# First RMS norm of a two-layer trunk: squares on VectorE, row scaling on ScalarE, and the high part of h written directly

## The chip, the cores and the metric

The kernel runs on one core of a Trainium2 chip. The metric is device time in microseconds (us) of one execution, median over runs. A core has a matrix engine (TensorE, in the profile PE, with its weight loads as PEld), VectorE (DVE), ScalarE (ACT), GpSimd (POOL), and a queue engine (SyncE, SP) that issues the loads here. Each engine works through its own list of instructions strictly in order; between engines they wait on semaphores. PSUM banks hold what TensorE writes; everything else is in SBUF.

## The reference

The model is one gated-MLP layer followed by one latent-attention layer, over 256 tokens of width 2048. The change touches the norm ahead of each sub-layer:

```python
def rms_norm(x, g):
    xf = x.astype(jnp.float32)
    y = xf * lax.rsqrt(jnp.mean(xf * xf, axis=-1, keepdims=True) + EPS)
    return (y * g.astype(jnp.float32)).astype(x.dtype)

def ada_mod(c, w, b):
    return (jax.nn.silu(c) @ w + b)[:, None, :]
...
    shift, scale, gate = jnp.split(ada_mod(c, ada_w[i], ada_b[i]), 3, axis=-1)
    h = rms_norm(x, norm_g[i]) * (1.0 + scale) + shift
    if i < N_A_LAYERS:
        out = gmlp_mixer(h, a_w_in[i], a_ln_g[i], a_ln_b[i], a_w_s[i], a_b_s[i], a_w_out[i])
...
    x = x + gate * out
```

`gmlp_mixer` begins with `h @ w_in`, a 2048 by 12288 product. The keys and values and the second layer take `h` in the same form.

## The kernel before

**Products.** Every matrix product is made in three passes of a reduced float format (fp32r): an operand is split into a high part `hi` and a rest `lo`, and hi by hi, lo by hi and hi by lo are summed. A weight piece of 1 MB (`raw`, two blocks of 128 rows by 1024 columns) is loaded by SP, cast to `hi` on ScalarE (L164) and subtracted to `lo` on VectorE (L166). It feeds 24 matmuls of 512 columns (L328): two row blocks, two token tiles, two halves of the columns, three passes.

**The left operand h.** `Norm.h` takes one block of 128 features of the transposed, normalised x (`xT`, in the second layer `zT`), applies the adaLN scale and shift as per-partition columns (L289, into a scratch tile `h` of which there are two), casts it to the high part (L290; the tile is called hh in the first layer, gh in the second, shi for the keys and values) and lets VectorE write the low part (L291; hl, gl, slo). It runs 52 times: 16 blocks in the first norm, 20 in the second (the first four blocks in two halves of 128 tokens), 16 for the keys and values.

**adaLN columns.** `Ada.step` loads 1 MB of transposed adaLN weights (`araw`) and VectorE multiplies it with silu(c), held as `s_b` on all partitions, and sums along the row (L191, one custom instruction and a short one that reads the accumulator). One step gives one column of 128 values. `modulate(k)` runs a shift step and a scale step and then `Norm.h` for block k, so a block of h costs 2 MB of loads. For the scale VectorE adds one and multiplies by the norm's weight (L195). The first steps, for blocks 0 and 1, are called sh0, sc0, sh1, sc1 below, and those for block 2 sh2 and sc2.

**The first norm.** `Norm.rows` handles one token tile of 128 rows after the other. ScalarE squares four quarters of a row with running sums (L145), VectorE adds the four sums (L158) and scales and shifts the mean (L139), GpSimd raises it to the power -0.5 (L140, tile `rs`), VectorE multiplies the four quarters with it (L262), and TensorE transposes each quarter (`flip`, L251) into a bank `px` from which ScalarE copies it to `xT` (L253). Two banks serve this. The two token tiles are called `x_83` and `x_85` in the lists below.

**Buffers and order.** Loads of `raw` and `araw` share four buffers of 1 MB: SP issues a load when VectorE has finished with the tile that was in its buffer. SP's order is that of the source; on the other engines a planner in the compiler sets the order of the instructions by costs of its own, so an edit in one place can move instructions elsewhere. The startup works in stages of 1, 1, 2, 2, 2 weight pieces per block of columns and calls `modulate` for the next stage between them.

**The second norm** (`norm1`) works otherwise: the transposes come first, and the row scales are applied to `zT` by VectorE from a transposed copy (`finish`, a PE transpose of `rs` at L275, and `scale`, L284; `zrb` is its copy in SBUF at L279). `early1` does blocks 0 to 3 for each token tile, `late1` the rest.

## Time and profile before

| what | value |
|---|---|
| median of 3 runs | 1158.75 us (1155.67 to 1169.34) |
| the profiled execution | 1158.37 us, of which the span from first to last instruction is 1156.6 us |
| granted TensorE clock, mean | 0.988 |
| TensorE busy | 1120.1 us (97% of the span) |
| VectorE busy | 958.4 us (83%) |
| ScalarE busy | 623.3 us (54%) |
| GpSimd busy | 53.9 us (5%) |
| DMA engines, share of the span on the loads' queue | 80% |

A row of a timeline gives the start in us, the time taken in us (from the start of the first to the end of the last where several are merged), the engine, the line, the operation, the tile written and the tiles read, their shapes and the count; in brackets stands how long the engine had been idle and what it waited for. A row of the windows gives the busy time of each engine in that stretch, then the granted TensorE clock, the busy share of the DMA engines, and GB/s.

### The profile page before, as it was taken

How to read it: one execution, taken by the hardware profiler on the slowest of the kernel's cores; microseconds unless marked ns; L12 is line 12 of the kernel's file. 1: busy time of each engine (PE TensorE's matmuls, PEld its weight loads, DVE VectorE, ACT ScalarE, POOL GpSimd, SP SyncE). 2: the span in 40 equal slices, each digit the busy share in tenths (PEclk: the TensorE clock that was granted, in tenths of full speed). 3: DMA queues.
4: the chain of work that ended last, by engine and by line, in shares of the span. 5: the costliest groups of instructions: out<-in, count | busy, mean ns of one | idle time of the engine just before them, and what ended most of it. 6: DMA issues, size and time to landing. Idle time of an engine off the chain costs nothing.

```text
span 1156.6 us, 14438 instructions
## 1 busy us (share of the span) xinstructions
PE 1120.1 (97%) x5148; PEld 919.3 (79%) x5148; DVE 958.4 (83%) x1389; ACT 623.3 (54%) x1150; POOL 53.9 (5%) x70
## 2 busy tenths in 40 slices
PE   7998999999999999999999989989999999999997
PEld 4777788888788888878888878868888788887886
DVE  6799999978998987897898888879876657687896
ACT  6744344456754434444445454457647688784332
POOL 0000000001210000000000000000000132120000
PEclk8999999999999999999999999989999999999999
DMA  9999888988898898989989989968986555245784
GB/s 354 350 344 344 309 316 329 339 295 299 301 350 338 320 345 317 357 308 348 361 306 339 335 293 339 326 246 328 359 297 196 200 155 165 84 163 199 259 301 188
DMA packets 80298, 338.30 MB, mean 292 GB/s; under 512 B 5729, under 2 KB 10209, under 8 KB 63457
## 3 DMA queue, kind: packets, MB, share of 16 engines
q1 hardware_dynamic: 79074, 335.29, 80.0%
q10 hardware_dynamic: 1152, 2.10, 0.6%
q8 instruction: 40, 0.66, 0.2%
q14 instruction: 32, 0.26, 0.1%
HBM read 335.26 MB, written 2.10 MB: 292 GB/s over the span
## 4 chain that ended last, share of the span: by engine, by line
PE 71%; DMA 10%; DVE 10%; issue 4%; ACT 4%; POOL 0%; SPq 0%; DVEq 0%; ACTq 0%; POOLq 0%
PE pm L328 58%; DMA araw<-in_ada_wT 4%; DVE lo L166 4%; PE pk L328 4%; PE pq L328 3%; DMA araw<-in_kv_ada_wT 3%; DVE araw L191 2%; ACT hi L164 1%; PE pS L845 1%; DMA raw<-in_a_w_in 1%; PE pS L844 1%; PE pmix L556 1%; ACT sq L145 1%; DMA lnb<-in_a_ln_b 1%; DVE v L467 1%
## 5 line engine op out<-in xcount | busy, mean ns | idle before, releaser
L164 ACT CAST hi<-raw 128x1024 fp32r<-128x1024 f32 (+2 forms) x376 | 382.2, 1029 | 403.2 <-PE pm L328 278.9
L166 DVE TENSOR_TENSOR lo<-raw,hi 128x1024 fp32r<-128x1024 f32 (+2 forms) x376 | 443.8, 1195 | 78.8 <-ACT hi L164 77.7
L191 DVE CUSTOM_DVE_ANT_0 araw<-araw,s_b,vec 128x2048 f32<-128x2048 f32 (+1 forms) x128 | 274.7, 2148 | 54.1 <-DMA araw<-in_ada_wT 33.6
L328 PE MATMUL pm<-lo,hh 128*128 128x512 f32 x768 | 251.9, 395 | 6.7 <-DVE lo L166 6.5
L328 PE MATMUL pm<-hi,hh 128*128 128x512 f32 x768 | 243.5, 394 | 6.6 <-ACT hh L290 3.5
L328 PE MATMUL pm<-hi,hl 128*128 128x512 f32 x768 | 247.9, 392 | 0.0
L328 PEld LDWEIGHTS pm<-lo,hh 128*128 128x128 f32 x768 | 143.8, 189 | 40.3 <-DVE lo L166 11.4
L328 PEld LDWEIGHTS pm<-hi,hh 128*128 128x128 f32 x768 | 145.0, 189 | 38.6 <-DVE v L467 4.1
L328 PEld LDWEIGHTS pm<-hi,hl 128*128 128x128 f32 x768 | 144.9, 189 | 30.8 <-DVE hl L291 0.3
L328 PE MATMUL pm<-lo,shi 128*128 128x512 f32 (+1 forms) x320 | 94.2, 371 | 2.3 <-DVE lo L166 2.3
L328 PE MATMUL pm<-hi,shi 128*128 128x512 f32 (+1 forms) x320 | 94.3, 374 | 0.9 <-ACT shi L164 0.9
L328 PE MATMUL pm<-hi,slo 128*128 128x512 f32 (+1 forms) x320 | 94.2, 372 | 0.0
L328 PEld LDWEIGHTS pm<-lo,shi 128*128 128x128 f32 x320 | 58.4, 188 | 12.6 <-DVE lo L166 2.7
L328 PEld LDWEIGHTS pm<-hi,shi 128*128 128x128 f32 x320 | 58.0, 188 | 11.0 <-ACT shi L164 1.3
L328 PEld LDWEIGHTS pm<-hi,slo 128*128 128x128 f32 x320 | 58.0, 188 | 10.0
L328 PE MATMUL pm<-hi,gh 128*128 128x512 f32 x160 | 52.9, 402 | 1.2 <-ACT kn L732 1.2
L328 PE MATMUL pm<-hi,gl 128*128 128x512 f32 x160 | 54.0, 400 | 0.0
L328 PE MATMUL pm<-lo,gh 128*128 128x512 f32 x160 | 53.5, 401 | 0.0
L328 PE MATMUL pk<-hi,latkv 128*128 128x512 f32 x128 | 43.9, 411 | 0.0
L328 PE MATMUL pm<-lo,ybh 128*128 128x512 f32 x128 | 43.2, 395 | 0.0
L328 PE MATMUL pm<-hi,ybl 128*128 128x512 f32 x128 | 43.0, 395 | 0.0
L328 PE MATMUL pm<-hi,ybh 128*128 128x512 f32 x128 | 42.9, 402 | 0.0
(178 smaller groups left out, 1240.4 us busy)
## 6 DMA issues: line engine op xcount, KB each, us to landing
araw<-in_ada_wT SPq DMA_DIRECT2D x96, 1024.0 KB, 6.5
raw<-in_a_w_in SPq DMA_DIRECT2D x96, 1024.0 KB, 6.6
raw<-in_a_w_out SPq DMA_DIRECT2D x32, 1024.0 KB, 7.2
araw<-in_kv_ada_wT SPq DMA_DIRECT2D x32, 1024.0 KB, 6.9
raw<-in_b_w_in SPq DMA_DIRECT2D x16, 1024.0 KB, 6.2
raw<-in_b_w_out SPq DMA_DIRECT2D x16, 1024.0 KB, 5.4
raw<-in_kv_w_ukv SPq DMA_DIRECT2D x8, 1024.0 KB, 5.6
raw<-in_b_w_uq SPq DMA_DIRECT2D x8, 768.0 KB, 4.9
```

The costliest lines, as they stand in the source:

```text
L145: nc.scalar.activation(j, src, AF.Square, scale=scale, accum_out=dst)
L164: nc.scalar.copy(hi, src)
L166: nc.vector.tensor_tensor(out=lo, in0=src, in1=hi.bitcast(F32), op=ALU.subtract)
L191: nc.vector.tensor_tensor_reduce(out=t[:, c], in0=t[:, c], in1=s_b[:, c], scale=1.0, scalar=acc, op0=ALU.mult, op1=ALU.add, accum_out=dst)
L328: nc.tensor.matmul(ps[i][:, :widths[i]], lhsT=lt, rhs=rhs[:, offs[i]:offs[i] + widths[i]], start=(first and c == 0 and which == 0 and rhs ...
L467: nc.vector.tensor_tensor(out=p, in0=ps, in1=p, op=ALU.add)
L556: nc.tensor.matmul(pmix[:, j * 256:(j + 1) * 256], lhsT=wsh["T"][:, g, :], rhs=piece(vt[i], t, n)[:, j * 256:(j + 1) * 256], start=True, s ...
L844: nc.tensor.matmul(pS[:, c0:c1], lhsT=qT[:, j, t * P:(t + 1) * P], rhs=kT[:, j, 0:nk], start=True, stop=False)
L845: nc.tensor.matmul(pS[:, c0:c1], lhsT=qrT[pb:pb + DR, t * P:(t + 1) * P], rhs=krT[pb:pb + DR, 0:nk], start=False, stop=True)
```

## The change

In `Norm.rows` both token tiles are now handled together. The squares of a whole row of 2048 are formed and summed by one VectorE instruction per tile, of the same kind as the adaLN step: it reads the row tile twice, as both inputs, and writes the products to a tile `sq` that nobody reads. The sum of four partial sums goes away. The rows are scaled on ScalarE, with the GpSimd result as a per-partition scale, quarter by quarter and both tiles in turn, and each quarter is transposed as before.

In `Norm.h` the high part is written first and straight from `xT` or `zT` with scale and shift; `h` itself is written by a second instruction of the same form, where a cast stood before. The low part is `h` minus the high part as before. This holds for all 52 uses.

```diff
-        def rows(self, t):
-
+        def rows(self):
+
+            r = []
+            for t in range(NT):
+                nc.vector.tensor_tensor_reduce(out=slot("sq"), in0=self.xt[t], in1=self.xt[t], scale=1.0, scalar=0.0, op0=ALU.mult, op1=ALU.add, accum_out=self.st[t][:, 0:1])
+                r.append(rstd_sum(self.st[t], 1, D))
             for q in range(4):
-                self.sums(t, q)
-            r = rstd_sum(self.st[t], 4, D)
-            for q in range(4):
-                x = self.xt[t][:, q * 512:(q + 1) * 512]
-                nc.vector.tensor_scalar_mul(x, x, r)
-                self.flip(t, q)
+                for t in range(NT):
+                    x = self.xt[t][:, q * 512:(q + 1) * 512]
+                    nc.scalar.activation(x, x, AF.Identity, scale=r[t])
+                    self.flip(t, q)
...
         def h(self, n, k, hi, lo, t0=0, t1=S):
             src = self.ts[k // 8][:, (k % 8) * S + t0:(k % 8) * S + t1]
+            scale, bias = ada["sc" + n].col[:, k:k + 1], ada["sh" + n].col[:, k:k + 1]
+            nc.scalar.activation(hi, src, AF.Identity, scale=scale, bias=bias)
             h = scratch([P, S], "h", "h")[:, :t1 - t0]
-            nc.scalar.activation(h, src, AF.Identity, scale=ada["sc" + n].col[:, k:k + 1], bias=ada["sh" + n].col[:, k:k + 1])
-            nc.scalar.copy(hi, h)
+            nc.scalar.activation(h, src, AF.Identity, scale=scale, bias=bias)
             return nc.vector.tensor_tensor(out=lo, in0=h, in1=hi.bitcast(F32), op=ALU.subtract)
...
-    for t in range(NT):
-        norm0.rows(t)
+    norm0.rows()
```

In the lists that follow, the lines of the changed kernel are two or three higher from L264 on (the scaling of the rows is L264 there, the squares L259, the high part L291, h L293, the low part L294). ISA is the custom VectorE instruction and the read of its accumulator.

**VectorE at the start, before:**

```order
L158 TENSOR_REDUCE ss_131<-st_121 128x1
L139 TENSOR_SCALAR rs_133<-ss_131 128x1
L262 TENSOR_SCALAR x_83<-x_83,rs_134 128x512 x4
L158 TENSOR_REDUCE ss_173<-st_122 128x1
L139 TENSOR_SCALAR rs_175<-ss_173 128x1
L191 ISA araw,col_sh_111<-araw,s_b,vec 128x2048
L191 ISA col_sh_111 128x1
L262 TENSOR_SCALAR x_85<-x_85,rs_176 128x512 x4
L191 ISA araw,col_sc_112<-araw,s_b,vec 128x2048
L191 ISA col_sc_112 128x1
L195 SCALAR_TENSOR_TENSOR col_sc_112<-col_sc_112,vec 128x1
L166 TENSOR_TENSOR lo<-raw,hi 128x1024 x2
```

And in the changed kernel, up to the first low part of h:

```order
L259 ISA sq,st_121<-x_83 128x2048
L259 ISA st_121 128x1
L139 TENSOR_SCALAR rs_125<-st_121 128x1
L259 ISA sq,st_122<-x_85 128x2048
L259 ISA st_122 128x1
L139 TENSOR_SCALAR rs_131<-st_122 128x1
L191 ISA araw,col_sh_111<-araw,s_b,vec 128x2048
L191 ISA col_sh_111 128x1
L191 ISA araw,col_sc_112<-araw,s_b,vec 128x2048
L191 ISA col_sc_112 128x1
L195 SCALAR_TENSOR_TENSOR col_sc_112<-col_sc_112,vec 128x1
L294 TENSOR_TENSOR hl_193<-h,hh_191 128x256
```

The second square stands directly behind the small operation (L139) whose result GpSimd waits for. The list goes on before, from the two low parts of the first weight piece, as

```order
L166 TENSOR_TENSOR lo<-raw,hi 128x1024 x2
L191 ISA araw,col_sh_111<-araw,s_b,vec 128x2048
L191 ISA col_sh_111 128x1
L291 TENSOR_TENSOR hl_209<-h,hh_207 128x256
L191 ISA araw,col_sc_112<-araw,s_b,vec 128x2048
```

and changed as

```order
L166 TENSOR_TENSOR lo<-raw,hi 128x1024
L191 ISA araw,col_sh_111<-araw,s_b,vec 128x2048
L191 ISA col_sh_111 128x1
L166 TENSOR_TENSOR lo<-raw,hi 128x1024
L191 ISA araw,col_sc_112<-araw,s_b,vec 128x2048
```

so the adaLN step sh1 has moved between the two low parts of the first weight piece, and the low part of h ahead of both.

**ScalarE at the start, before:**

```order
L128 ACTIVATE s_b<-pc 128x512
L145 ACTIVATE sq,st_121<-x_83 128x512 x4
L128 ACTIVATE s_b<-pc 128x512 x2
L145 ACTIVATE sq,st_122<-x_85 128x512 x4
L128 ACTIVATE s_b<-pc 128x512
L253 COPY xT_119<-px 128x4x128 x2
L253 COPY xT_120<-px 128x4x128 x2
L253 COPY xT_119<-px 128x4x128 x2
L253 COPY xT_120<-px 128x4x128 x2
L164 CAST hi<-raw 128x1024 x2
L289 ACTIVATE h<-xT_119,col_sh_111,col_sc_112 128x256
L290 CAST hh_207<-h 128x256
```

and changed:

```order
L128 ACTIVATE s_b<-pc 128x512 x3
L264 ACTIVATE x_83<-x_83,rs_126 128x512 x4
L128 ACTIVATE s_b<-pc 128x512
L253 COPY xT_119<-px 128x4x128
L264 ACTIVATE x_85<-x_85,rs_132 128x512 x4
L253 COPY xT_119<-px 128x4x128 x3
L253 COPY xT_120<-px 128x4x128
L291 ACTIVATE hh_191<-xT_119,col_sh_111,col_sc_112 128x256
L293 ACTIVATE h<-xT_119,col_sh_111,col_sc_112 128x256
L164 CAST hi<-raw 128x1024 x2
L253 COPY xT_120<-px 128x4x128 x3
```

The last quarter of `s_b`, which the first adaLN step needs whole, now stands behind the four scalings of the first tile; the first block of h stands ahead of the first weight cast and of three transposed quarters.

**ScalarE at the second norm, before,** from the first copy of the row scales on:

```order
L279 COPY zrb<-px 128x128
L289 ACTIVATE h<-zT_232,col_sh_114,col_sc_115 128x128 x2
L253 COPY zT_233<-px 128x4x128
L290 CAST gh_5866<-h 128x128 x2
L279 COPY zrb<-px 128x128
L289 ACTIVATE h<-zT_232,col_sh_114,col_sc_115 128x128 x2
L290 CAST gh_5866<-h 128x128 x2
L289 ACTIVATE h<-zT_232,col_sh_114,col_sc_115 128x128 x2
L290 CAST gh_5866<-h 128x128 x2
L289 ACTIVATE h<-zT_232,col_sh_114,col_sc_115 128x128 x2
L290 CAST gh_5866<-h 128x128 x2
```

and changed:

```order
L281 COPY zrb<-px 128x128
L291 ACTIVATE gh_5850<-zT_216,col_sh_114,col_sc_115 128x128
L293 ACTIVATE h<-zT_216,col_sh_114,col_sc_115 128x128
L291 ACTIVATE gh_5850<-zT_216,col_sh_114,col_sc_115 128x128
L293 ACTIVATE h<-zT_216,col_sh_114,col_sc_115 128x128
L291 ACTIVATE gh_5850<-zT_216,col_sh_114,col_sc_115 128x128 x2
L253 COPY zT_217<-px 128x4x128
L293 ACTIVATE h<-zT_216,col_sh_114,col_sc_115 128x128 x2
L281 COPY zrb<-px 128x128
L291 ACTIVATE gh_5850<-zT_216,col_sh_114,col_sc_115 128x128 x4
L291 ACTIVATE shi<-zT_216,col_shk,col_sck 128x256 x2
L293 ACTIVATE h<-zT_216,col_sh_114,col_sc_115 128x128 x4
```

High parts no longer need one of the two `h` tiles, so they run ahead; the four `h` of the second token tile now stand behind six high parts, two of which (shi) are for the keys and values. SP's order is the same in both kernels.

## The prediction

> **What bounds the kernel now.** I read the windows by stage first, then the chain of waits, then the timelines of VectorE, ScalarE and GpSimd over the first 36 us.

> ```profile
> 0.00:43.00 43.00, 34.15 (x113) 22.81 (x114) 28.64 (x40) 28.59 (x54) 2.48 (x11) 0.92 0.94 363
> 43.00:75.00 32.00, 32.00 (x143) 26.50 (x142) 27.46 (x30) 20.23 (x31) 0.00 (x0) 1.00 0.95 346
> 75.00:124.00 49.00, 42.86 (x174) 33.09 (x172) 47.65 (x58) 18.28 (x23) 0.00 (x0) 0.97 0.89 326
> 124.00:400.00 276.00, 274.45 (x1214) 226.22 (x1215) 246.78 (x281) 147.07 (x205) 15.00 (x19) 1.00 0.89 322
> ...
> 5.99 2.51 ACT sq L145 x8
> 124.08 135.99 PE pm L328 x598
> ```

> The columns after the length are PE, PEld, VectorE, ScalarE and GpSimd, then clock, DMA share and GB/s. From 43 to 75 us TensorE is never idle; from 75 to 124 VectorE is (47.65 of 49 us busy) what it waits for; from 124 on the chain is matmuls. So the end moves with TensorE's stream: whatever the first 40 us gain or lose is passed on, unless VectorE's slack (28.64 of 43 us busy) takes it up. The first 18 us of the chain are what the change rewrites; the first squares on ScalarE (5.99) head it.

> **The first norm.** These rows carry the start:

> ```profile
> 1.61 0.42 SPq L114 DMA_DIRECT2D x<-in_x  x1
> x<-in_x SPq DMA_DIRECT2D x1, 1024.0 KB, 6.9
> 8.45 1.05 ACT L128 ACTIVATE s_b<-pc 128x512 f32<-128x512 f32 x2
> 8.77 0.15 DVE L139 TENSOR_SCALAR rs<-ss 128x1 f32<-128x1 f32 x1
> 9.01 0.56 POOL L140 TENSOR_TENSOR rs<-rs,nhalf 128x1 f32<-128x1 f32 x1 [7.17 <-DVE rs L139]
> 9.60 1.67 DVE L262 TENSOR_SCALAR x<-x,rs 128x512 f32<-128x512 f32 x4 [0.68 <-POOL rs L140]
> 11.86 0.58 ACT L128 ACTIVATE s_b<-pc 128x512 f32<-128x512 f32 x1
> 12.47 2.35 DVE L191 CUSTOM_DVE_ANT_0 araw<-araw,s_b,vec 128x2048 f32<-128x2048 f32 x1
> 18.60 0.08 DVE L191 DVE_READ_ACCUMULATOR2_ANT col_sc<- 128x1 f32 x1
> 18.72 0.16 DVE L195 SCALAR_TENSOR_TENSOR col_sc<-col_sc,vec 128x1 f32<-128x1 f32 x1
> 22.04 1.22 PE L328 MATMUL pm<-hi,hh 128*128 128x512 f32 x2 [3.50 <-ACT hh L290]
> 27.49 2.36 DVE L166 TENSOR_TENSOR lo<-raw,hi 128x1024 fp32r<-128x1024 f32 x2
> 29.78 2.35 DVE L191 CUSTOM_DVE_ANT_0 araw<-araw,s_b,vec 128x2048 f32<-128x2048 f32 x1
> L489 ACT ACTIVATE vj<-v,vmu 128x512 f32<-128x512 f32 x16 | 11.4, 713 | 0.0
> ```

> Removed are eight squares on ScalarE and eight scalings on VectorE. Added are two VectorE instructions of the adaLN kind, 2.35 us each by the row at 12.47, and eight ScalarE scalings, for which the row of L489 (same shape, a per-partition operand) gives 0.71 us each; back to back they overlap by about 0.1, as two s_b take 1.05 us (8.45) and one takes 0.58 (11.86). I take 0.6 us a step, 2.5 us for four.

> The first square runs 5.99 to 8.34 us. The small L139 follows at about 8.38, and GpSimd starts 0.24 us after that (8.77 to 9.01), at 8.62. The second row tile lands at 1.61 + 6.9 = 8.51 us, so VectorE starts the second square at about 8.53, just ahead of GpSimd. What that costs is shown elsewhere in the trace:

> ```profile
> 332.17 2.35 DVE L166 TENSOR_TENSOR lo<-raw,hi 128x1024 fp32r<-128x1024 f32 x2
> 332.34 2.60 POOL L140 TENSOR_TENSOR rs<-rs,nhalf 128x1 f32<-128x1 f32 x1 [10.53 <-DVE rs L139]
> 293.01 2.34 DVE L191 CUSTOM_DVE_ANT_0 araw<-araw,s_b,vec 128x2048 f32<-128x2048 f32 x1
> 293.16 2.30 POOL L644 TENSOR_TENSOR rs<-cs,gr 128x32 f32<-128x32 f32 x1
> 288.40 0.25 POOL L643 TENSOR_TENSOR rc<-cs,gr 128x32 f32<-128x32 f32 x1
> 12.41 0.56 POOL L140 TENSOR_TENSOR rs<-rs,nhalf 128x1 f32<-128x1 f32 x1 [2.69 <-DVE rs L139]
> ```

> The same power took 2.60 us when VectorE had begun a two-input operation 0.17 us earlier, and ended 0.42 us after VectorE did (334.52 to 334.94). A 0.25 us GpSimd product took 2.30 us beside an adaLN step. At 12.41 GpSimd was 0.06 us ahead and took its usual 0.56. So the first row scale comes at 8.53 + 2.35 + 0.42 = 11.3 us, not at 8.62 + 0.56 = 9.2. [...]

> From there, in ScalarE's new order: four scalings 11.3 to 13.8; the last quarter of s_b, now behind them, to 14.3 (before 12.44); VectorE's sh0 14.35 to 16.7 and sc0 to 19.05 (before 18.68); the scale column at 19.2 (before 18.88). ScalarE has by then copied one quarter (0.57), scaled the second tile (to 17.35) and copied four quarters at TensorE's pace to 19.95; hh 19.95 to 20.55, h to 21.05, the first two weight casts (1.0 each) to 22.0 and 23.0. TensorE's first matmul, which now waits for the first cast, is at 22.05: no change from 22.04. VectorE: hl 21.05 to 21.5, lo 22.05 to 23.2, sh1 to 25.5, lo to 26.65, sc1 to 29.0, two lo to 31.4. Before, those two ended at 29.85 (row at 27.49). The term is +1.55, say **+1.6 us**: the two scalings of 1.67 us that VectorE sheds are paid for by squares of 4.7 us and by starting the adaLN steps 1.9 us later.

> Bounds: with GpSimd first, the same walk from 9.2 instead of 11.3 puts the two lo at 29.4 (−0.45) and the first matmul at 20.0; if TensorE's start alone counted, −2.0. The other end is the load of sh2, which takes the buffer of the first weight piece:

> ```profile
> 22.52 0.33 SPq L183 DMA_DIRECT2D araw<-in_ada_wT  x1
> araw<-in_ada_wT SPq DMA_DIRECT2D x1, 1024.0 KB, 7.2
> 18.71 0.38 SPq L309 DMA_DIRECT2D raw<-in_a_w_in  x1
> 1.21 4.75 DMA x<-in_x
> ```

> It went out at 22.52 and landed at 29.72, just as VectorE took it (29.78). With sh1 between the two lo it goes out at 26.65. The only other load then under way, issued at 19.05 for 18.71, has landed, so I take the 4.75 us of the first x tile, an almost empty queue: 31.4, when VectorE is free. With 7.2 us it is 33.85, 4.1 us behind before. The row nearest in load is the first, so the sum takes +1.6 and the range keeps −2.0 and +4.1. SP's order and its loads don't change.

> **The high part first.** An h and a cast become two instructions of the first kind:

> ```profile
> L289 ACT ACTIVATE h<-xT,col_sh,col_sc x16: 593/602/633, 20.9 to 226.7; 128x256 f32<-128x256 f32 x16
> L290 ACT CAST hh<-h x16: 398/405/455, 21.6 to 228.5; 128x256 fp32r<-128x256 f32 x16
> 771.09 0.89 ACT L289 ACTIVATE h<-zT,col_sh,col_sc 128x128 f32<-128x128 f32 x2
> 772.48 0.48 PE L275 MATMUL px<-ident,rs 128*128 128x128 f32 x1 [1.99 <-ACT zT L253]
> 772.70 1.22 PE L328 MATMUL pm<-hi,gh 128*128 128x512 f32 x2
> 777.69 0.49 DVE L291 TENSOR_TENSOR gl<-h,gh 128x128 fp32r<-128x128 f32 x2 [0.93 <-ACT gh L290]
> 779.64 3.49 DVE L284 TENSOR_TENSOR zT<-zT,zrb 128x1024 f32<-128x1024 f32 x3
> 785.65 1.22 DVE L166 TENSOR_TENSOR lo<-raw,hi 128x1024 fp32r<-128x1024 f32 x1
> 787.16 0.61 PE L328 MATMUL pm<-lo,gh 128*128 128x512 f32 x2
> ```

> The high part comes 0.4 us earlier, the pair costs up to 0.2 us more, 52 times: 10 us of ScalarE, which is 54% busy (table above). TensorE waits for a high part of h once in the trace, 3.50 us at 22.04, counted above. Elsewhere I cost it at nothing, since TensorE is fed from stored h while ScalarE works; if that cover were gone it would be the 10 us. The place without cover is the second norm. There the first matmul need no longer stand behind the transpose of the second row scale (772.48, which waited for GpSimd): gh is ready at about 771.6, and TensorE starts 1.0 us earlier. But the h of the second token tile stand behind six high parts. Walking ScalarE from 771.09 at 0.40 us an instruction (0.49 each with 0.1 of overlap, since two take 0.89), and 0.55 for each shi: zT copied at 774.05, four gh to 776.8, two shi to 777.85, the first h of the second tile at 778.3. VectorE's gl for it comes at 778.35, not 777.69, the low part and two more gl behind it end at 780.65, and the three scalings of zT start 1.0 us later than 779.64. Behind those stand an adaLN step and the low part that before ran 785.65 to 786.87: now it ends at 787.6 (zT at 784.1, 2.34 of adaLN, 1.22), and the gl, which has moved behind the second low part, at 789.1, where before TensorE took the low part at 787.16 without a wait. That block of twelve matmuls ends near 790.0 instead of 789.0: **+1.0 us**. Bounds: −1.0 if TensorE keeps its earlier start, +2.5 if the six instructions take their full 0.49 and 0.60 and the gl waits that much longer. The low part was needed with nothing to spare, so I take +1.0.

> The sum: 1158.37 + 1.6 + 1.0 = **1161.0 us**. The profiled execution is 0.38 below the median of the runs, which I leave; two of the three runs differ by 3.1, so the median itself is good to a microsecond or so.

> **Rivals.**
> - GpSimd gets in first. The margin is 0.09 us, and the landing of x decides. Then 1158.37 − 0.45 + 1.0 = 1158.9. The row at 12.41 shows that 0.06 us is enough.
> - The earlier matmuls count: first matmul at 20.0 and 771.6, and VectorE's slack up to 75 us (27.46 of 32 us busy from 43 on) takes up the rest. 1158.37 − 2.0 − 1.0 = 1155.4. Against it, VectorE is the bound from 75 to 124 us.
> - Slower still, by the buffers: sh2 lands 4.1 us late and the second norm loses 2.5: 1165.0. It decides if a load into a queue with one other under way still takes 7 us, as in the row at 22.52.
> - ScalarE's 10 us are uncovered: 1168.3, from the point where TensorE waits for h in each of the 52. To be slower by over 2% each would have to cost 0.45 us, more than twice the row's price.

> **How the numbers follow.** Forecast 0.46, GpSimd first 0.25, earlier matmuls 0.12, late buffers 0.13, uncovered ScalarE 0.03 (a third of it beyond 2%); 0.01 is left for anything else. The forecast alone spans 1159.5 to 1163. The range, 1154 to 1166, holds all but the last cases, with a microsecond at each end for the scatter of the runs. Two per cent is 23 us, about what a measurement of this kernel can tell from no change; no case but one reaches it: faster 0.01, same 0.98, slower 0.01.

> **What would show it.** The first GpSimd power taking about 2.6 us and ending near 11.3; the last s_b near 14; the scale column near 19.2; first matmul near 22; the second pair of lo ending near 31.4. In the second norm, a first matmul a microsecond earlier relative to the squares ahead of it, VectorE idle for a microsecond or two before the gl of the second tile, and a new wait of TensorE for lo or gl some 15 us on. I am wrong if the first power takes 0.56 us, or if the planner's other small moves, in the startup near 35 to 60 us or after 886 us, open waits of their own, which I haven't priced.

## The result, and the profile after

The changed kernel took 1165.18 us (median of 20 runs, 1158.79 to 1170.28) against 1157.69 us (20 runs) of the kernel before beside it: a ratio of 1.0058, 95% interval 1.0039 to 1.0078, so +6.7 us (4.5 to 9.0) of about 1158; the two medians lie 7.5 apart, and differences below go by the ratio unless they say otherwise. That is no difference of 2%. The time lies in the predicted range near its upper end; the forecast was +2.6, so the direction is right and the size is not.

The profiled execution of the changed kernel took 1167.28 us, with a span of 1165.6 and a mean clock of 0.987. Its windows by stage; the first four are those shown of before, with the same columns (PE, PEld, VectorE, ScalarE, GpSimd, clock, DMA share, GB/s after the length):

```profile
0.00:43.00 43.00, 30.14 (x92) 19.41 (x93) 26.88 (x32) 24.35 (x40) 4.54 (x11) 0.92 0.87 344
43.00:75.00 32.00, 32.00 (x143) 26.46 (x142) 26.91 (x28) 22.73 (x35) 0.00 (x0) 1.00 0.86 317
75.00:124.00 49.00, 43.34 (x181) 34.43 (x180) 47.60 (x59) 19.01 (x23) 0.00 (x0) 0.97 0.89 334
124.00:400.00 276.00, 270.55 (x1190) 222.51 (x1190) 240.53 (x271) 145.03 (x201) 14.91 (x19) 0.99 0.87 315
...
769.00:801.00 32.00, 27.39 (x114) 21.17 (x112) 26.79 (x41) 28.84 (x58) 1.10 (x2) 0.89 0.51 184
```

In the first 43 us TensorE does 92 matmuls where it did 113. From 43 to 75 us it is busy all the time, as before: the second h instruction on ScalarE (22.73 us for 20.23) delays nothing there, and nothing is caught up either. From 75 to 124 VectorE is the bound as before. The second norm's stretch is new to this table; of the kernel before it reads:

```profile
769.00:801.00 32.00, 29.72 (x124) 24.34 (x125) 29.12 (x41) 22.98 (x50) 0.79 (x2) 0.89 0.64 234
```

The chain of the changed kernel in the first 31 us has the squares on VectorE, GpSimd's power and the scalings on ScalarE where the squares on ScalarE stood before:

```profile
6.02 2.29 DVE sq L259
...
8.59 2.67 POOL rs L140
...
11.29 1.95 ACT x L264 x4
```

To see where the time goes I number the 5148 matmuls (each trace has them all; the extra ones of E10 below are left out) and take, for the n-th, its start in one trace less its start in before's. For the changed kernel this is +4.65 us from n = 100 (40 us) to n = 250 (74 us), without a change in between; 6.19 at n = 3280, where the second norm's transposes begin; 7.69 at n = 3400, 31 us later; 7.70 at n = 3850 (886 us); 8.95 at the end. So it loses 4.65 at the start, 1.50 in the second norm and 1.25 from 886 us on, each read from this one execution. The 1.5 between 74 and 769 us I don't count: two kernels below whose instructions stand in the same order up to there differ by more than that.

**The start.** The timeline of the changed kernel over all engines, the first 36 us:

```profile
8.35 0.15 DVE L139 TENSOR_SCALAR rs<-st 128x1 f32<-128x1 f32 x1
8.55 2.29 DVE L259 CUSTOM_DVE_ANT_0 sq<-x 128x2048 f32<-128x2048 f32 x1
8.59 2.66 POOL L140 TENSOR_TENSOR rs<-rs,nhalf 128x1 f32<-128x1 f32 x1 [6.75 <-DVE rs L139]
11.29 2.56 ACT L264 ACTIVATE x<-x,rs 128x512 f32<-128x512 f32 x4 [2.49 <-POOL rs L140]
13.75 0.57 ACT L128 ACTIVATE s_b<-pc 128x512 f32<-128x512 f32 x1
14.36 2.35 DVE L191 CUSTOM_DVE_ANT_0 araw<-araw,s_b,vec 128x2048 f32<-128x2048 f32 x1 [3.32 <-ACT s_b L128]
...
22.35 1.19 PE L331 MATMUL pm<-hi,hh 128*128 128x512 f32 x4 [0.81 <-ACT hi L164]
...
27.79 0.73 PE L331 MATMUL pm<-hi,hh 128*128 128x512 f32 x2 [1.62 <-ACT hi L164]
29.34 2.36 DVE L166 TENSOR_TENSOR lo<-raw,hi 128x1024 fp32r<-128x1024 f32 x2
30.62 1.22 PE L331 MATMUL pm<-lo,hh 128*128 128x512 f32 x2 [2.10 <-DVE lo L166]
31.64 1.05 PE L331 MATMUL pm<-hi,hl 128*128 128x512 f32 x2
```

VectorE's second square begins 0.04 us ahead of GpSimd's power, and the power takes 2.66 us. Everything to 29.34 follows from that as forecast. What wasn't forecast is in the last two rows: two matmuls take 1.05 us, where in the same place before they took 0.62. The windows of the changed kernel show the clock (the column after GpSimd):

```profile
20.00:26.00 6.00, 5.12 (x24) 3.59 (x22) 4.10 (x5) 4.21 (x7) 0.00 (x0) 1.00 0.69 254
26.00:30.00 4.00, 0.90 (x4) 0.30 (x2) 3.96 (x5) 3.02 (x5) 0.00 (x0) 0.87 0.78 262
30.00:34.00 4.00, 3.38 (x8) 2.71 (x9) 4.00 (x5) 0.55 (x2) 0.00 (x0) 0.50 1.01 414
34.00:38.00 4.00, 4.00 (x15) 3.18 (x15) 2.74 (x4) 0.77 (x2) 0.00 (x0) 0.77 1.03 416
```

and those of before:

```profile
20.00:26.00 6.00, 3.96 (x9) 3.14 (x10) 5.87 (x6) 2.59 (x5) 0.00 (x0) 0.54 0.94 339
26.00:30.00 4.00, 3.16 (x11) 2.23 (x10) 3.96 (x6) 2.36 (x4) 0.00 (x0) 0.84 0.97 336
30.00:34.00 4.00, 4.00 (x18) 3.11 (x17) 4.00 (x4) 0.93 (x2) 0.00 (x0) 1.00 0.97 354
```

Both kernels have nearly 7 us at half clock by this column (a window at 0.50 is half clock throughout, one at 0.77 for 46% of it). Before, most of that came while TensorE was going to wait for the low parts of VectorE anyhow; now most comes behind that wait, when the matmuls have all that they need. By the trace's clock records the changed kernel's clock falls at 28.98 us, inside the second of the two waits, and is back at 35.81. With the windows cut there:

```profile
25.57:28.98 3.41, 1.33 (x7) 0.65 (x5) 3.41 (x4) 2.48 (x3) 0.00 (x0) 1.00 0.64 192
28.98:32.40 3.42, 1.78 (x4) 1.49 (x5) 3.38 (x6) 1.09 (x2) 0.00 (x0) 0.50 1.01 419
32.40:35.81 3.41, 3.41 (x9) 2.64 (x9) 3.41 (x4) 0.00 (x0) 0.00 (x0) 0.50 0.99 402
```

TensorE worked 1.33 of the 3.41 us ahead of the fall. The last section says why the cuts are made there.

**The second norm.** TensorE and ScalarE of the changed kernel:

```profile
777.84 1.22 PE L331 MATMUL pm<-hi,gh 128*128 128x512 f32 x2 [1.11 <-ACT gh L291]
...
792.95 4.05 ACT L291 ACTIVATE gh<-zT,col_sh,col_sc 128x256 fp32r<-128x256 f32 x8
793.32 1.20 PE L331 MATMUL pm<-lo,gh 128*128 128x512 f32 x4 [0.73 <-DVE lo L166]
794.79 0.74 PE L331 MATMUL pm<-hi,gl 128*128 128x512 f32 x2 [0.27 <-DVE gl L294]
796.90 1.04 ACT L164 CAST hi<-raw 128x1024 fp32r<-128x1024 f32 x1
...
801.07 0.73 PE L331 MATMUL pm<-hi,gl 128*128 128x512 f32 x2 [0.51 <-DVE gl L294]
```

The first matmul comes 5.14 us later than before's (772.70) in a stream that is 6.19 late, so 1.05 earlier. Then there are three waits that the kernel before doesn't have, and a row of eight high parts on ScalarE, 4 us long, between two weight casts. Behind the first of these waits, at n = 3350, the changed kernel has given the early start back and lost 0.67; the other 0.83 of the 1.50 come from there to n = 3400.

**From 886 us.** Here the first latent of the keys and values is scaled. VectorE and TensorE of the changed kernel:

```profile
896.50 0.15 DVE L158 TENSOR_REDUCE ss<-ss 128x1 f32<-128x2 f32 x1
897.26 1.22 DVE L166 TENSOR_TENSOR lo<-raw,hi 128x1024 fp32r<-128x1024 f32 x1 [0.61 <-ACT hi L164]
898.40 0.14 DVE L139 TENSOR_SCALAR rs<-ss 128x1 f32<-128x1 f32 x1
899.83 0.48 PE L699 MATMUL px<-ident,cn 128*128 128x128 f32 x1 [4.01 <-ACT cn L695]
```

and of before:

```profile
888.78 0.15 DVE L158 TENSOR_REDUCE ss<-ss 128x1 f32<-128x2 f32 x1
888.96 0.15 DVE L139 TENSOR_SCALAR rs<-ss 128x1 f32<-128x1 f32 x1
...
890.40 0.44 PE L697 MATMUL px<-ident,cn 128*128 128x128 f32 x2 [2.28 <-ACT cn L693]
```

The planner has put a low part, which itself waits for its cast, between the sum and the row scale that TensorE waits for. The transposes behind it wait 4.01 us instead of 2.28.

### The profile page after: what moved, and what is told of

Its sections match the earlier page's. It is cut to its first block, busy times and chain, and to the rows that moved or that the text cites. A ratio compares the mean times of both kernels' runs of the same rounds, so it can differ in the third digit from the quotient of the medians.

```text
span 1165.6 us, 14419 instructions
## 1 busy us (share of the span) xinstructions
PE 1121.8 (96%) x5148; PEld 920.7 (79%) x5148; DVE 959.6 (82%) x1383; ACT 629.5 (54%) x1142; POOL 55.8 (5%) x70
## 4 chain that ended last, share of the span: by engine, by line
PE 78%; DVE 10%; DMA 6%; ACT 3%; issue 3%; POOL 1%; DVEq 0%; SPq 0%; ACTq 0%; POOLq 0%
PE pm L331 64%; DVE lo L166 4%; DMA araw<-in_ada_wT 4%; PE pk L331 4%; PE pq L331 3%; DVE araw L191 3%; PE pS L847 1%; DMA raw<-in_a_w_in 1%; PE pmix L558 1%; PE pS L846 1%; ACT hi L164 1%; DVE v L469 1%; PE pt L565 1%; PE pT L864 0%; DMA araw<-in_kv_ada_wT 0%
## 5 line engine op out<-in xcount | busy, mean ns | idle before, releaser
L166 DVE TENSOR_TENSOR lo<-raw,hi 128x1024 fp32r<-128x1024 f32 (+2 forms) x376 | 443.0, 1193 | 72.7 <-ACT hi L164 71.6
L191 DVE CUSTOM_DVE_ANT_0 araw<-araw,s_b,vec 128x2048 f32<-128x2048 f32 (+1 forms) x128 | 274.6, 2147 | 66.6 <-DMA araw<-in_ada_wT 48.6
## 6 DMA issues: line engine op xcount, KB each, us to landing
araw<-in_ada_wT SPq DMA_DIRECT2D x96, 1024.0 KB, 6.8
raw<-in_a_w_in SPq DMA_DIRECT2D x96, 1024.0 KB, 6.8
raw<-in_a_w_out SPq DMA_DIRECT2D x32, 1024.0 KB, 7.3
araw<-in_kv_ada_wT SPq DMA_DIRECT2D x32, 1024.0 KB, 6.7
raw<-in_b_w_in SPq DMA_DIRECT2D x16, 1024.0 KB, 6.6
raw<-in_b_w_out SPq DMA_DIRECT2D x16, 1024.0 KB, 5.6
raw<-in_kv_w_ukv SPq DMA_DIRECT2D x8, 1024.0 KB, 5.6
```

Of the source, the lines that this page charges most:

```text
L166: nc.vector.tensor_tensor(out=lo, in0=src, in1=hi.bitcast(F32), op=ALU.subtract)
L191: nc.vector.tensor_tensor_reduce(out=t[:, c], in0=t[:, c], in1=s_b[:, c], scale=1.0, scalar=acc, op0=ALU.mult, op1=ALU.add, accum_out=dst)
```

## The experiments

Three sets of four kernels were run, each beside the kernel before on the same chip. The theories were these. First A, that the late start (GpSimd's power) costs nearly all, against B, that the high part first and what the planner makes of it costs most. After the first set C, that three places add up: the start, the second norm, and the latent near 890 us; against D, that one of these is an accident of single executions. For the last set C was made sharper, on the clock in the start and on high parts that run ahead in the second norm, against E, that the order of the low parts and the length of the pair cost the time. The labels run from E1 to E14; no kernel is called E3 or E13.

The table has all of them. "Start" is the lateness at n = 250 (74 us), "norm" what is added from n = 3280 to 3400, "end" what is added from n = 3850 to the last; each from one trace against before's. "Sum" adds the three; "time" is the measured ratio less 1, times 1158 us. Under "first" stands whether the second square or GpSimd was first in that profile.

| kernel | first norm | h | first | start | norm | end | sum | ratio, 95% interval | time, us |
|---|---|---|---|---|---|---|---|---|---|
| changed | new | new | square | +4.65 | +1.50 | +1.25 | +7.4 | 1.0058 [1.0039, 1.0078] | +6.7 |
| E1 | new | old | GpSimd | −0.41 | +0.26 | −0.07 | −0.2 | 1.0031 [1.0008, 1.0055] | +3.6 |
| E2 | old | new | – | +0.45 | +2.30 | +1.51 | +4.3 | 1.0043 [1.0020, 1.0065] | +5.0 |
| E4 | new, GpSimd forced first | new | GpSimd | +2.66 | +2.32 | +1.51 | +6.5 | 1.0057 [1.0029, 1.0086] | +6.6 |
| E5 | as E4, last s_b forced first | new | GpSimd | +2.98 | +4.12 | +1.04 | +8.1 | 1.0079 [1.0049, 1.0110] | +9.1 |
| E6 | new | old in the first norm | square | +1.37 | +2.27 | +1.03 | +4.7 | 1.0061 [1.0031, 1.0091] | +7.1 |
| E7 | old | new in the second norm | – | +0.14 | +1.70 | −0.11 | +1.7 | 1.0033 [1.0002, 1.0064] | +3.8 |
| E8 | new, GpSimd forced first | old | GpSimd | −0.32 | −0.06 | −1.63 | −2.0 | 0.9999 [0.9968, 1.0031] | −0.1 |
| E9 | old | new in the first norm | – | +2.02 | +0.23 | +0.01 | +2.3 | 1.0006 [0.9977, 1.0035] | +0.7 |
| E10 | new | new, TensorE kept busy | GpSimd | +0.40 | +1.48 | +1.47 | +3.4 | 1.0041 [1.0016, 1.0065] | +4.7 |
| E11 | old | second norm, in turn | – | +1.42 | −0.80 | −0.04 | +0.6 | 0.9989 [0.9971, 1.0007] | −1.3 |
| E12 | new | new, all in turn | square | +3.51 | −0.29 | +0.98 | +4.2 | 1.0034 [1.0015, 1.0054] | +3.9 |
| E14 | as E8 | second norm, in turn | GpSimd | −0.32 | −0.85 | −1.61 | −2.8 | 1.0004 [0.9981, 1.0028] | +0.5 |

Between 74 and 769 us the traces move by several us without a reason in the code: E12 has the changed kernel's order up to there, yet from n = 250 to 3280 it gains 3.84 where the changed kernel loses 1.54; E7 has that of before and loses 3.02. Where one was followed, the 2.35 us that the changed kernel loses near 266 us of its trace, it was a wait for a load that landed late (7.30 us, in the chain of waits); the others were not all followed. They differ from one execution to the next. So a sum of three places and a measured time are compared only to within some us; the column "norm", where each kernel's waits are seen directly, is sharper. All three columns also hold what the clock did in that one execution: in the second norm the changed kernel and the one before had 6.83 us at half clock, E11 and E12 3.41, E7 and E14 none.

### E1 and E2: one half of the change alone

E1 has the new first norm and the old h; E2 the old first norm and the new h:

```diff
-            nc.scalar.activation(hi, src, AF.Identity, scale=scale, bias=bias)
             h = scratch([P, S], "h", "h")[:, :t1 - t0]
             nc.scalar.activation(h, src, AF.Identity, scale=scale, bias=bias)
+            nc.scalar.copy(hi, h)
```

That is E1 against the changed kernel, without the line that names scale and bias; E2 is the kernel before with the reverse of it.

> The first norm's part alone (squares on VectorE, scaling on ScalarE); h and its cast as before. Theory A (the late first row scale and the late adaLN steps of the start cost nearly all, and the delay of the loads carries it on): +4 to +6 us against before, first GpSimd power about 2.6 us, second pair of lo ending near 31.7 us, fortieth microsecond of TensorE's stream 3 to 5 us late. Theory B (the high part written first, and the instructions that the planner moved for it, cost most): +1 to +3 us, the delay at the start absorbed by 130 us.

> The high part first alone; the first norm as before. Theory A: +0 to +2 us, no difference up to 40 us, about 1 us lost in the second norm. Theory B: +4 to +6 us.

E1 took +3.6 us (0.9 to 6.4) and E2 +5.0 (2.3 to 7.5). A asked for 0 to 2 of E2 and falls; B holds for E2. E1's time separates nothing: it lies between B's 1 to 3 and A's 4 to 6, and its interval holds much of both. (The expectation of E8 below calls it +2.0, the difference of the medians.) E1's profile has something else that matters. GpSimd and VectorE at the start of E1:

```profile
8.61 0.56 POOL L140 TENSOR_TENSOR rs<-rs,nhalf 128x1 f32<-128x1 f32 x1 [6.77 <-DVE rs L139]
8.70 2.29 DVE L259 CUSTOM_DVE_ANT_0 sq<-x 128x2048 f32<-128x2048 f32 x1 [0.18 <-DMA x<-in_x]
```

VectorE waited 0.18 us for the second tile of x, so its square began 0.15 us later than in the changed kernel's profile; GpSimd came first and needed its usual 0.56 us. The code is the same up to there. Of the five profiles here in which the second square isn't held back, it was first in three (the changed kernel, E6, E12) and GpSimd in two (E1, E10). So the runs of one kernel are a mixture of both cases, and E1's time need not be that of its profile.

### E4 and E5: GpSimd made first

E4 is the changed kernel, but the second square adds a zero that GpSimd forms from its first power, so it can't start before that. E5 also issues the scalings of x behind the last quarter of s_b.

E4 against the changed kernel:

```diff
-            r = []
+            r, zero = [], 0.0
             for t in range(NT):
-                nc.vector.tensor_tensor_reduce(out=slot("sq"), in0=self.xt[t], in1=self.xt[t], scale=1.0, scalar=0.0, op0=ALU.mult, op1=ALU.add, accum_out=self.st[t][:, 0:1])
+                nc.vector.tensor_tensor_reduce(out=slot("sq"), in0=self.xt[t], in1=self.xt[t], scale=1.0, scalar=zero, op0=ALU.mult, op1=ALU.add, accum_out=self.st[t][:, 0:1])
                 r.append(rstd_sum(self.st[t], 1, D))
+                if t == 0:
+                    zero = sml.tile([P, 1], F32, tag="zero", name="zero")
+                    nc.gpsimd.tensor_tensor(out=zero, in0=r[0], in1=r[0], op=ALU.subtract)
```

E5 against E4 (sb_last is the last instruction that writes s_b):

```diff
-                    nc.scalar.activation(x, x, AF.Identity, scale=r[t])
+                    with behind(sb_last):
+                        nc.scalar.activation(x, x, AF.Identity, scale=r[t])
```

> The changed kernel, with the second square made to wait for the first GpSimd power (its starting value is a zero that GpSimd forms from that power), so that GpSimd gets in first; the same result, one more small GpSimd instruction. Theory A: the first power takes 0.56 us and ends near 9.2, the last s_b ends near 12.3 instead of 14.3, sc0 near 17.0 instead of 19.0, second pair of lo near 29.7 instead of 31.7; time +2 to +4 us against before where the changed kernel has +6.7. Theory B: the start is as early, the time stays at +5 to +7.

> As the run before, and the last quarter of s_b is queued ahead of the scalings of x on ScalarE. Theory A: sh0 starts near 11.7 (behind the second square) and sc0 ends near 16.3; -1 to +2 us against before. Theory B: +4 to +6.

In E4 the start is 2.0 us earlier than in the changed kernel (+2.66 for +4.65): that is the price of the power held up by the square, 2.66 us for 0.56. The time doesn't show it (+6.6 for +6.7, with intervals of ±3 and ±2), as is to be expected if part of the changed kernel's runs have GpSimd first anyhow. E5 gained nothing by its earlier adaLN steps: A asked for −1 to +2, B for +4 to +6, and it got +9.1 (5.7 to 12.7). Its profile has no half clock from 20 to 100 us and is still at +2.98 at 74 us. There the planner set the weight casts of the second pair behind a copy of transposed x that waits 3.68 us for TensorE, so that the pair of low parts starts at 29.51 us for 27.36 in E4. A late start need not be the clock.

### E6 to E9: the high part first at one place

E6 is the changed kernel with this in h:

```diff
-            scale, bias = ada["sc" + n].col[:, k:k + 1], ada["sh" + n].col[:, k:k + 1]
-            nc.scalar.activation(hi, src, AF.Identity, scale=scale, bias=bias)
-            h = scratch([P, S], "h", "h")[:, :t1 - t0]
-            nc.scalar.activation(h, src, AF.Identity, scale=scale, bias=bias)
+            if n != "0":
+                scale, bias = ada["sc" + n].col[:, k:k + 1], ada["sh" + n].col[:, k:k + 1]
+                nc.scalar.activation(hi, src, AF.Identity, scale=scale, bias=bias)
+                h = scratch([P, S], "h", "h")[:, :t1 - t0]
+                nc.scalar.activation(h, src, AF.Identity, scale=scale, bias=bias)
+            else:
+                h = scratch([P, S], "h", "h")[:, :t1 - t0]
+                nc.scalar.activation(h, src, AF.Identity, scale=ada["sc" + n].col[:, k:k + 1], bias=ada["sh" + n].col[:, k:k + 1])
+                nc.scalar.copy(hi, h)
```

E7 is the kernel before with the condition n == "1" (the second norm), E9 the kernel before with n == "0" (the first). E8 is E4 with the old h everywhere.

> The changed kernel with the old pair (h, then its cast) in the first norm's h alone; the second norm and the keys and values keep the high part first. Theory C (three places add up: the high part first at the start about 3 us together with the late first row scale, in the second norm 1.5 to 2.3, and 1.2 to 1.5 more near 890 us where the rows of the latent are scaled): the stream stands between -0.5 and +1.5 us against before at 40 us and goes on so to 769 us but for waits for late loads, loses 1.5 to 2.3 by 800 us and 1.2 to 1.5 by 901; time +3 to +5 against before, 2 to 3 less than the changed kernel. Theory D (the start's order is innocent, and the 4.65 us at 40 us come from the late first row scale and TensorE's lower clock there, whatever the order of h): +4 to +5 us at 40 us if the second square starts ahead of GpSimd, and a time within 1 us of the changed kernel's.

> The kernel before with the high part first in the second norm alone. Theory C: nothing moves to 769 us; first matmul of the second norm about 1 us earlier, then waits that leave the stream 1.5 to 2.3 us behind at 800 us; what it loses near 890 us shows whether that belongs to the second norm's order (1.2 to 1.5) or to the keys' and values' h (0); time +1.5 to +3.5. Theory D (TensorE's earlier start in the second norm pays for most of the later waits, and the 2.3 us seen are of one execution): 0 to +1 at 800 us, time 0 to +1.

> The changed first norm with the old h everywhere, and the second square made to wait for a zero that GpSimd forms from the first power, so that GpSimd is first each time. Theory C: first row scale at about 9.3 us, the low parts of the second pair of weights end at 29.3 to 29.6, first matmul 2 us earlier than before, the stream 0.4 to 2 us ahead at 40 us and no waits of its own in the second norm or near 890 us; time -2 to +1 against before, and below the kernel that has the changed first norm with the old h without the zero (+2.0 measured). Theory D (the rows part costs by itself what is not seen in the start, since loads that start earlier or later collide): +2 to +4 as that kernel.

> The kernel before with the high part first in the first norm's h alone. Theory C: the old first norm leaves the start's order of h little to lose: 0 to +1.5 us at 40 us, nothing in the second norm or near 890 us; time 0 to +2. Theory D (the order of h at the start costs 3 us by itself, also without the new first norm): +2.5 to +3.5 at 40 us and the same in the time.

The places come apart. In the second norm every kernel with the high part first there, in whatever order the planner likes, loses 1.5 to 4.1 us (seven kernels), and every one with the old h between −0.06 and +0.26 (three). From 886 us on the six with the high part first for the keys and values (changed, E2, E4, E5, E6 and E10 below) lose 1.0 to 1.5; E7, which has it in the second norm alone, loses nothing there, nor do E1 and E9. So that loss belongs to the h of the keys and values, and the planner's order there, not to the second norm: in all six, and in E12 below, a low part stands between the two small instructions, in the others not. E8 gains 1.6, as E14 below does, and that is the clock: from 892 to 896 us the clock granted to E8 is 1.00 and it starts 20 matmuls, where before has 0.72 and 15; E14's records have no half clock from 805 to 912 us either. E5, E6 and E12 lose some 2.6 us up to 905 us and regain 1.6 at a half clock near 930 us that before has and they have not. So the 1.0 to 1.5 of this column are not a price to a tenth; the longer wait for the transposes is 1.7 us in the changed kernel (4.01 for 2.28).

The start: with the old h it is +1.37 when the square is first (E6) and −0.32 when GpSimd is (E8). With the high part first it is +4.65 and +2.66 (E4). So in these executions the late power costs 1.7 to 2.0, and the high part first 3.0 to 3.3 on top; E12 below, which has the changed kernel's order and the square first, but 3.41 us at half clock there for 6.83, is at +3.51, which makes it 2.1. With the old first norm it has no fixed price: E9 is at +2.02, and E2, whose instructions stand in the same order up to the second norm, at +0.45. In E9 the clock was 0.50 from 26 to 30 and 0.64 from 30 to 34 us, in E2 0.80 and 1.00. By the trace's clock records it fell at 22.62 us in E9 and stayed at half for 10.24, in E2 at 20.75 for 6.83. D's "3 us by itself" falls, but C's 0 to 1.5 was too little for E9.

C was too low for the time of E6 (+3 to +5, measured +7.1, 3.6 to 10.5), right for E8 and E9, and 0.3 too low for E7 (1.5 to 3.5, measured +3.8, 0.2 to 7.4). By the times alone the intervals of E7 and E8 also hold what D asked; what speaks against D is the places.

### E10: TensorE kept busy in the start

The changed kernel with 20 transposes whose result nobody reads, where TensorE waits at 26 us. On every engine the order of all other instructions is the same.

```diff
+            d = bank("pc")
+            for j in range(20):
+                nc.tensor.transpose(d[:, j % 4 * P:(j % 4 + 1) * P], self.xt[1][:, (j % 4) * P:(j % 4 + 1) * P], ident)
```

> The changed kernel with 20 further transposes of x into a bank that nobody reads, behind TensorE's last four transposes of the start (about 26.2 us), where it waits for a high and a low part of the weights; every other instruction stands where it stood. Theory C (of the 4.65 us at 40 us, 2 to 3 are the lower clock that the two idle stretches of 1.6 and 2.1 us bring on, while matmuls wait): the clock stays at 1.0 from 30 to 36 us, the first copy of v comes near 34.5 instead of 37.23, and the stream stands at +1.5 to +2.5 us at 40 us; time 2 to 3 us below the changed kernel's. Theory E (the lateness comes from the order of the low parts and h in VectorE and ScalarE, and the clock only fills the wait): the clock stays up, but the stream is within 1 us of the changed kernel's +4.65 at 40 us.

GpSimd came first in this profile, so the kernel to set beside it is E4, not the changed one. Windows of E10:

```profile
26.00:30.00 4.00, 2.18 (x11) 1.49 (x10) 3.97 (x6) 1.61 (x3) 0.00 (x0) 1.00 1.00 385
30.00:34.00 4.00, 4.00 (x19) 3.14 (x18) 4.00 (x4) 1.25 (x3) 0.00 (x0) 1.00 0.98 378
```

and of E4:

```profile
26.00:30.00 4.00, 1.88 (x5) 1.24 (x5) 3.97 (x6) 1.77 (x3) 0.00 (x0) 0.63 1.02 395
30.00:34.00 4.00, 4.00 (x11) 3.08 (x10) 4.00 (x4) 0.00 (x0) 0.00 (x0) 0.52 0.98 385
```

From 30 to 34 us both are busy all the time, one with 19 matmuls and the other with 11. In E10 the matmuls of the low part start at 28.47 us, behind a wait of 1.82, and the first copy of v at 32.75; in E4 at 28.63, behind 2.12, and 35.24:

```profile
28.47 0.73 PE L335 MATMUL pm<-lo,hh 128*128 128x512 f32 x2 [1.82 <-DVE lo L166]
...
32.75 2.05 ACT L475 COPY v<-pm 128x512 f32<-128x512 f32 x4 [4.35 <-PE pm L335]
```

```profile
28.63 1.22 PE L334 MATMUL pm<-lo,hh 128*128 128x512 f32 x2 [2.12 <-DVE lo L166]
...
35.24 2.05 ACT L474 COPY v<-pm 128x512 f32<-128x512 f32 x4 [6.68 <-PE pm L334]
```

At 74 us E10 is at +0.40 and E4 at +2.66. With the windows cut as above for the changed kernel, E10 reads

```profile
24.86:28.27 3.41, 1.79 (x15) 1.36 (x12) 3.38 (x4) 2.62 (x4) 0.00 (x0) 1.00 0.88 332
```

and the clock stayed up behind 1.79 us of work, where E4's fell behind 1.31 and the changed kernel's behind 1.33. So between these two executions 2.26 of the 3 us that the high part first costs at the start are the clock (0.16 of it an earlier low part), and C holds; E, that the clock only fills the wait, falls. The clock isn't the order's alone, though: E11 below has the start of the kernel before, instruction for instruction, and is at +1.42 with a clock of 0.69 from 30 to 34 us, where E7 with the same start is at +0.14. E7's clock fell once, for 6.83 us from 21.21; E11's twice, for 3.41 from 22.22 and again from 29.05. What the profiles show is how often it hits: of the nine with at most one half of the change at the start (before among them) it made two late (E9, E11); of the three with both halves and E10's or E5's edits not in them (the changed kernel, E4, E12) all three. In the time E10 is 2 us below the changed kernel, as C said, though within the intervals.

### E11, E12, E14: high part and h in turn

Each high part is issued behind the h before it, so no more than two high parts stand in a row:

```diff
-            nc.scalar.activation(hi, src, AF.Identity, scale=scale, bias=bias)
+            with behind(self.last):
+                nc.scalar.activation(hi, src, AF.Identity, scale=scale, bias=bias)
             h = scratch([P, S], "h", "h")[:, :t1 - t0]
-            nc.scalar.activation(h, src, AF.Identity, scale=scale, bias=bias)
+            self.last = nc.scalar.activation(h, src, AF.Identity, scale=scale, bias=bias)
```

E11 has it in the second norm on the kernel before, E12 in all three norms on the changed kernel, E14 in the second norm on E8.

> The kernel before with the high part first in the second norm alone, and each high part issued behind the h before it, so that ScalarE writes high part, h, high part, h, and never eight high parts in a row ahead of a weight cast. Theory C (the 1.7 to 4.1 us that the second norm loses come from high parts that no longer wait for a free h and run ahead of the weight casts): no stretch of more than two high parts, no wait of TensorE for lo above 1 us between 780 and 801 us, the stream -1 to +0.7 us over the stretch from the last matmul before the norm to 30 us on; time -1.5 to +1 against before. Theory E (the loss comes from the pair's greater length, 1.1 us for 0.9, and from the h of the second token tile standing behind high parts): +1 to +2 over that stretch, as without the forced order, and the same in the time.

> The changed kernel with each high part issued behind the h before it in all three norms. Its start has the changed kernel's order, so +4 to +5 us at 40 us, or about 2 us less where GpSimd gets in ahead of the second square. Theory C: the second norm loses -1 to +0.7 instead of 1.5 to 2.3; near 890 us a low part still stands between the two small instructions of the latent's row scale, so 1 to 1.5 are lost there; time 1.5 to 2.5 below the changed kernel's. Theory E: the second norm loses 1 to 2.3 as before; time within 1 us of the changed kernel's.

> The changed first norm with GpSimd made first by the zero from its first power, the old h in the first norm and for the keys and values, and in the second norm the high part first with each high part behind the h before it. Theory C: the start of the kernel with the zero and the old h (-0.3 us at 40 us), the second norm at -1 to +0.7, nothing near 890 us; time -2.5 to +0.5 against before, the lowest of all kernels here or level with before. Theory E: 1 to 2 slower than the kernel with the zero and the old h, so +0.5 to +2 against before.

The second norm now gains: −0.80, −0.29 and −0.85 where E7 and the changed kernel lost 1.70 and 1.50. TensorE of E12 over the second norm, its waits:

```profile
771.32 1.22 PE L333 MATMUL pm<-hi,gh 128*128 128x512 f32 x2 [1.16 <-ACT gh L293]
...
785.84 1.20 PE L333 MATMUL pm<-lo,gh 128*128 128x512 f32 x4 [1.00 <-DVE lo L166]
787.31 0.73 PE L333 MATMUL pm<-hi,gl 128*128 128x512 f32 x2 [0.28 <-DVE gl L296]
```

The earlier first matmul is still there, and the first wait for a low part too; what is gone is what came behind it. From n = 3350 to 3400 (786 to 797 us in E12) the three lose 0.00 to 0.02 us; the changed kernel lost 0.83 there, E2 1.19, E7 2.55. Up to n = 3350 part of the difference is the clock. E7 and E14, both at full clock through the whole stretch, leave it out: at n = 3350 they are level, at −0.84 and −0.85, and from there E7 loses 2.55 and E14 nothing.

How that loss arises shows on VectorE, in E7 and then in E14:

```profile
793.20 2.35 DVE L191 CUSTOM_DVE_ANT_0 araw<-araw,s_b,vec 128x2048 f32<-128x2048 f32 x1 [2.13 <-DMA araw<-in_kv_ada_wT]
```

```profile
793.75 3.49 DVE L166 TENSOR_TENSOR lo<-raw,hi 128x1024 fp32r<-128x1024 f32 x3
```

Between its two adaLN steps for the keys and values VectorE has four low parts in E14, as in E11, E12 and the kernels with the old h, and no wait for the second step's load. In the changed kernel, E2, E4, E6 and E10 it has three and waits 0.95 to 1.03 us, in E5 and E7 two and waits 2.08 and 2.13: with eight high parts ahead of the weight casts the planner sets low parts behind the adaLN step, VectorE reaches that step before its load has landed, and the low parts come late.

E11 and E7 differ only in this order: −1.3 us (−3.4 to +0.8) against +3.8 (0.2 to 7.4). E12, +3.9, is 2.8 below the changed kernel; the intervals overlap, and its start has less half clock, so it is the places that speak against E: the second norm loses nothing where E asked for 1 to 2.3. C's start of +4 to +5 for E12 was too much (+3.51). E12 still loses 0.98 from 886 us on, as expected, since its planner leaves the low part between the two small instructions.

None of these is shown to beat the kernel before. E11 has the lowest median (1156.15 us), with an interval that reaches over 1; E14, which should have been lowest by its places, came to +0.5 (−2.2 to +3.2), which both theories allow.

## Why the prediction was right or wrong

**GpSimd held by the second square: right, in some runs.** The square was put at 8.53 and the power at 8.62, and came at 8.55 and 8.59. The power ended at 11.25 for 11.3 and cost 2.66 us. It ended 0.41 us behind the square (8.55 + 2.29 = 10.84); in the row of before at 332.34, from which the cost was taken, the power had ended 0.42 behind VectorE. The rival that GpSimd gets in first was given 0.25; it came true in two of five profiles, with the landing of x as the reason that was given. Neither case sets the time alone. For GpSimd first the prediction put the end of the second pair of low parts at 29.4 (by its own step of 2.1 us it would be 29.3), and E10 has 29.55.

**The walk to 31.4: right to 0.3 us.** Last s_b to 14.32 (14.3), sh0 from 14.36 (14.35), scale column 19.18 (19.2), first matmul 22.35 (22.05), the pair of low parts to 31.70 (31.4). The load of sh2, taken at 31.4 with a bound at 33.85, kept nobody waiting: VectorE took it at 31.62, straight behind the low parts. So the rival of late buffers has no part in it.

**The term +1.6 for the start: the step that failed.** It set the lateness of the stream equal to that of the low parts on VectorE ("The term is +1.55, say +1.6"). For the new first norm that holds: E6, with the old h, is at +1.37. But the stream came to +4.65, and the other 3.3 belong to the high part first, which in the prediction was "counted above" for the first h and nothing elsewhere. In the planner's order for it TensorE has done the first weight piece's matmuls and the last transposes by 26.2 us at full clock and stands idle for 1.62 and 2.10 us, with one pair of matmuls between, just before the low parts come; the clock is at half when they do. E10 gives 2.26 us for that, though the clock's moment varies between executions of one order. The remainder of about 0.7 (E10 +0.40 against E8 −0.32) I didn't take apart.

**Nothing elsewhere for ScalarE's longer pair: right.** From n = 100 to 250 the lateness doesn't change by 0.01 us. The rival of 10 uncovered us is out.

**The second norm: right in kind, too small in size, and half wrong in cause.** The first matmul 1.0 us earlier (1.05, against its stream), VectorE idle for 1 to 2 us before the second tile's gl (1.71), and a new wait of TensorE for lo and gl some 15 us on (15.5 us behind the first matmul) all came. The term was +1.0 with a bound of +2.5, and measured 1.50 in the changed kernel, 1.5 to 4.1 in the seven that share it. It was worked out from h that stand behind six high parts, and from the pair's length. Up to the first wait for a low part that is about what came: 0.67 in the changed kernel. The other 0.83 are those of eight high parts in a row ahead of a weight cast, which the walk of ScalarE didn't reach, since it ended at the second tile's h: VectorE has a low part less to do and waits 0.98 us for an adaLN load. E11, E12 and E14 keep the longer pair and don't have this loss.

**The planner's small moves: named, not priced.** "After 886 us" was one of the two places where the prediction said it would be wrong. One such move cost 1.0 to 1.5 us. The rival that the earlier matmuls count is out: in the second norm the early start of 1.05 is there, and is given back 15 us later.

The places make 4.65 + 1.50 + 1.25 = 7.4 us, within the interval of what was measured, 4.5 to 9.0; forecast were 1.6 + 1.0. With the runs a mixture of both orders at the start, an estimate of some 1 us less (two of five profiles, 2.0 us each) is to be expected of the first.

That the stated range holds the time is in part luck: its upper end came from a late load of sh2 (4.1 us), for which nothing waited, beside 2.5 us in the second norm. What filled it instead was the clock at the start, with which the prediction doesn't reckon.

## What to carry to other kernels

A matmul that may start earlier isn't a gain by itself: ask what TensorE waits for next, and whether an idle stretch of a few us now stands right ahead of the burst that bounds the stage, since in the changed kernel the clock fell there (waits of 1.62 and 2.10 us, clock at 0.50 from 28.98 to 35.81 us). When a value no longer needs a scarce buffer, its writers run ahead as far as the planner lets them; a work order that holds them in turn with their partners kept the early start here without the later waits. Where two engines start within 0.1 us of each other and the order sets how long one of them takes, as here (the power 2.66 us when it began 0.04 behind the square, 0.56 in E1, where it began 0.09 ahead), expect both outcomes among the runs, and don't read a price from one profile.

## What the runs showed of the hardware

```profile
9.13 1.91 POOL L646 TENSOR_TENSOR gqk<-vec 128x1 f32<-128x1 f32 x1
```
